# A delta rule loop by token halves: TensorE's order laid out by strands with dense products in their waits, norms by one-column products, a decay mask by a product

## Chip, cores and metric

The kernel runs on one core of one Trainium2 chip, in one launch. The metric is the device time of that core in microseconds (us), the median of several executions.

## What is computed

A trunk of two layers over 1024 tokens of width 1024, all in float32. Layer 0 mixes tokens with gated linear attention (GLA), layer 1 with a gated delta rule; behind each mixer stands a SwiGLU feed-forward part, and a root-mean-square norm stands ahead of each part and at the end. The change lies in the delta rule mixer:

```python
proj = h @ w_in
qkv, z, b, a = split(proj)
qkv = silu(causal_depthwise_conv(qkv, conv_w))
q, k, v = split(qkv)            # 8 heads of q and k, 16 of v, 128 wide
q, k = l2_norm(q), l2_norm(k)
...
# for each chunk of tokens, with S carried from chunk to chunk:
decay = exp(where(causal, G[:, None] - G[None, :], -inf))
A = where(strict, (kb @ k.T) * decay, 0)
T = triangular_solve(eye + A, eye)
v_new = T @ (v * beta) - (T @ (kb * exp(G))) @ S
o = (q * exp(G)) @ S + where(causal, (q @ k.T) * decay, 0) @ v_new
S = exp(G_last) * S + k_dec.T @ v_new
...
return (rms_norm(o, norm_w) * silu(z)) @ w_out
```

## The kernel before

**Precision.** A large product ("dense") takes each operand as a high and a low part in the fp32r type and makes three products of 512 columns, high by high, high by low and low by high (`mm3`, recorded at lines 153 to 155 whatever the stage). Weights come by DMA on SyncE's queue (SP) into a buffer `raw` (2), ScalarE casts the high part `whi` (line 122), GpSimd subtracts to get the low part `wlo` (line 123); there are 3 buffers for the split parts. Small products are plain fp32 and show as two records each.

**Units.** The delta rule stage, `gdn`, works in 16 units: two halves of 512 tokens by 8 head pairs, each with one q, one k and two v heads, and 4 chunks of 128 tokens. A half's normed input (`normx`) and its gates are made once. For each unit:

- *keys*, *values*, *late*: dense products of 24 each for q and k, v0 and v1, and the two halves of the gate z; q, k and v go through a convolution on VectorE (line 588) and a Silu on ScalarE.
- *prep*: products k by k (line 618), transposes of q (621), squares and norms from both (627, 628, `rsqrt`), the decay matrix dec (GpSimd makes rh at 654, TensorE multiplies it at 655, ScalarE takes Exp at 656, GpSimd multiplies by the triangular mask at 657), the score matrix nt (663, one buffer) and at (676, 678). Four diagonal blocks of nt go by DMA through DRAM into nbx (670, 672).
- *solve*: transposes of k and v (kt at 696, vt at 704), then 31 steps of two VectorE operations each (712, 714) that invert the diagonal blocks; the result goes by DMA through DRAM into xt (719, 722).
- *join*: four steps of products (737) with copies between them make the whole inverse tt (730 to 750, one buffer).
- *seq*: the recurrence over 4 chunks with the state gstate (766 to 813), where TensorE, VectorE and ScalarE alternate.
- *post*: a second `rsqrt`, transposes of o (825), the gate (`gateout`, lines 264 to 266); *out*: 48 dense products that are added to h (240).

**Order.** `pipeline` writes one iteration after another as a list of steps with offsets, here "solve+1 seq late+1 keys+2 out-1 prep+2 values+2 post join+1". The framework's scheduler then orders the instructions of every engine by its own estimate of when they are ready, in favour of those written first. On the chip each engine runs its instructions in that order, and waits where one isn't ready. At the end `ffnhead` begins the next feed-forward part ahead of the last unit's post.

PSUM is in three pools: `pd` (3 banks) for dense products, `pp` (2) for preparation, `pq` (3) for join, seq and post.

Of the kernel before, what the change touches and what calls it, by code (L numbers as in the profile page):

```python
# [32 lines left out]
HEAD = 3  # L33

# [17 lines left out]

class Trunk:
    def __init__(self, ctx, tc, a):
        self.ctx, self.tc, self.nc, self.a = ctx, tc, tc.nc, a
        nc = tc.nc
# [17 lines left out]
    def mixerpools(self, es):  # L74

        pool = lambda nm, n: es.enter_context(self.tc.tile_pool(name=nm, bufs=n))
        self.wr, self.ws, self.tp = pool("wraw", 2), pool("wsplit", 3), pool("units", 2)
        self.xs = self.tc.tile_pool(name="xhalf", bufs=1, side="right")
        self.xp = self.xs.__enter__()
# [17 lines left out]
    def loadrest(self):  # L97
# [13 lines left out]
        nc.vector.tensor_copy(self.gt, g)  # L111

# [37 lines left out]

    def mm3(self, ps, lhs, rhs, first, last, **kw):
        mm = self.nc.tensor.matmul
# [4 lines left out]
    def chan(self, ps, w, c0, x, ks=range(KT)):  # L157

        for k in ks:
            self.mm3(ps, [t[:, k, c0:c0 + P] for t in w], [t[:, k, :] for t in x], k == 0, k == ks[-1],  # L160
                     skip_group_check=ks[0] > 0)

# [6 lines left out]
    def rsqrt(self, s, n):  # L169
# [27 lines left out]
    def normx(self, half, w, pool, scratch, tag="jk"):  # L197

        nc = self.nc
        hi = pool.tile([P, KT, HT], F32R, name="xhi", tag="xhi")  # L200
        lo = pool.tile([P, KT, HT], F32R, name="xlo", tag="xlo")
        r = self.normr(half, lambda i: scratch.tile([P, HT], F32, name="jk", tag=tag, bufs=2))
        for k in range(KT):
# [3 lines left out]
            eng.tensor_tensor(out=xn, in0=src, in1=r.unsqueeze(2).to_broadcast([P, C, P]), op=ALU.mult)  # L207
            ps = self.prepps()
            for t in range(C):
                nc.tensor.transpose(ps[:, t * P:(t + 1) * P], xn[:, t, :], self.ident)  # L210
            self.split(hi[:, k, :], lo[:, k, :], ps, w[:, k:k + 1])
        return hi, lo
# [18 lines left out]
    def addout(self, half, w, lhs, cc):  # L231

        if True:
            for t in range(C):
                ps = self.dps()
                for k in range(2):
                    self.mm3(ps, [v[:, t * P:(t + 1) * P] for v in lhs[k]],
                             [v[:, k, :] for v in w], k == 0, k == 1)
                o = self.h[:, half * C + t, cc * 512:(cc + 1) * 512]
                self.nc.vector.tensor_tensor(out=o, in0=o, in1=ps, op=ALU.add)  # L240
# [13 lines left out]
    def outproj(self, half, w, r0, oT):  # L254
        for cc in range(2):
            self.addout(half, self.loadrows(w, r0, cc), oT, cc)
# [242 lines left out]
    def gdn(self, tail):  # L499
# [3 lines left out]
        NQ, B = 8, 32  # L503
        with ExitStack() as es:
            self.mixerpools(es)
# [22 lines left out]
            def gates(x):  # L528

                low = mx.tile([2 * B, HT], F32, name="low", tag="raw", bufs=2)  # L530
                S.copy(low, self.lowproj(w_in, 6 * D, B, x)[0:2 * B, :])
                ps = self.prepps()
                for t in range(C):
                    TE.matmul(ps[:, t * B:(t + 1) * B], low[:, t * P:(t + 1) * P], two, start=True, stop=True)
# [3 lines left out]
                tmp6 = mx.tile([P, 6, C, 16], F32, name="tmp6", tag="raw", bufs=2)  # L538
# [24 lines left out]
                flat = lambda t: t.rearrange("p c h -> p (c h)")  # L563
                ps = self.prepps()
                TE.matmul(ps[:, 0:64], self.upper, flat(g), start=True, stop=True)
# [603 lines left out]
```

## Time and profile before

| | |
|---|---|
| median of 3 runs | 3312.93 us (3312.15 to 3317.28) |
| profiled execution, its own time | 3317.64 us |
| profiled execution, span from first to last instruction | 3315.9 us |
| TensorE products busy / weight loads busy | 2979.9 us (90%) / 2422.4 us (73%) |
| VectorE / ScalarE / GpSimd busy | 2174.2 us (66%) / 1386.2 us (42%) / 1564.2 us (47%) |
| mean granted TensorE clock | 0.958 |

Times inside a profile are counted from the span's start. PE is TensorE's products, PEld its weight loads, DVE VectorE, ACT ScalarE, POOL GpSimd, SP the queue of SyncE that issues the DMAs. The granted clock is the mean of TensorE's two levels as a share of the full one: 1 is 2.4 GHz throughout, 0.5 would be 1.2 GHz throughout. The delta rule stage lies between about 1251 and 2690 us.

### The profile page before, as it was taken

The page shows a single profiled execution, that of the slowest core. Times are in us where ns is not written, and L with a number is a line of the kernel's source. Part 1 is how long each engine was busy: PE and PEld are TensorE (multiplying, and loading weights), DVE is VectorE, ACT ScalarE, POOL GpSimd, SP SyncE. Part 2 cuts the span into 40 slices and gives each one's busy share as a digit, 9 for nine tenths or more (in the row PEclk, how much of TensorE's full clock was granted, in tenths as well). Part 3 has the DMA queues.
Part 4 walks back from the last instruction along what each step waited for, and adds up shares of the span by engine and source line. Part 5 has one row for each costly group of instructions (what it writes and reads, how often), then busy time and mean ns, then how long its engine had stood idle before and what let it go on. Part 6 is the DMA issues. An engine that isn't in the chain of part 4 may idle for free. (4 is left out here: it accounts for less than half of the span.)

```text
span 3315.9 us, 40871 instructions
## 1 busy us (share of the span) xinstructions
PE 2979.9 (90%) x14323; PEld 2422.4 (73%) x14323; DVE 2174.2 (66%) x4493; ACT 1386.2 (42%) x2605; POOL 1564.2 (47%) x1069
## 2 busy tenths in 40 slices
PE   6988989799998999788898988899988889999898
PEld 5877877578886777677676766777776678887676
DVE  6465665633225996768888888888878542232998
ACT  5345444334343334444444544444444433333333
POOL 4344443455556874433333333333432355554885
PEclk9999999899999999899999999999999999999999
DMA  4222212322223312222222222222222232222331
GB/s 127 73 59 58 70 58 78 107 83 83 83 77 121 111 67 53 69 61 59 62 69 63 53 74 63 65 76 68 63 68 60 70 111 81 85 83 82 138 104 58
DMA packets 364924, 256.40 MB, mean 77 GB/s; under 512 B 67847, under 2 KB 309966, under 8 KB 364718
## 3 DMA queue, kind: packets, MB, share of 16 engines
q1 hardware_dynamic: 364654, 253.77, 25.8%
q8 instruction: 113, 1.85, 0.2%
q14 instruction: 93, 0.76, 0.1%
q0 software_dynamic: 64, 0.02, 0.0%
HBM read 219.12 MB, written 34.60 MB: 77 GB/s over the span
## 5 line engine op out<-in xcount | busy, mean ns | idle before, releaser
L123 POOL TENSOR_TENSOR wlo<-raw,whi 128x1024 fp32r<-128x1024 f32 x204 | 490.2, 2405 | 842.7 <-ACT whi L122 716.9
L153 PE MATMUL pd<-xhi,whi 128*128 128x512 f32 x1072 | 442.8, 414 | 0.9 <-ACT xhi L193 0.9
L154 PE MATMUL pd<-xlo,whi 128*128 128x512 f32 x1072 | 437.1, 408 | 0.0
L155 PE MATMUL pd<-xhi,wlo 128*128 128x512 f32 x1072 | 434.0, 405 | 0.0
L122 ACT CAST whi<-raw 128x1024 fp32r<-128x1024 f32 x204 | 214.0, 1049 | 295.0 <-issue 119.2
L895 POOL TENSOR_TENSOR olo<-s,ohi 128x512 fp32r<-128x512 f32 x152 | 195.9, 1290 | 206.1 <-ACT ohi L894 206.1
L895 POOL TENSOR_TENSOR olo<-raw,ohi 128x512 fp32r<-128x512 f32 x138 | 190.3, 1382 | 209.3 <-ACT ohi L894 181.7
L155 PEld LDWEIGHTS pd<-xhi,wlo 128*128 128x128 f32 x1072 | 205.6, 192 | 39.6 <-issue 0.3
L153 PEld LDWEIGHTS pd<-xhi,whi 128*128 128x128 f32 x1072 | 206.2, 193 | 38.7 <-ACT xhi L193 1.4
L154 PEld LDWEIGHTS pd<-xlo,whi 128*128 128x128 f32 x1072 | 206.6, 193 | 37.1
L153 PE MATMUL pd<-whi,ohi 128*128 128x512 f32 x384 | 164.5, 429 | 35.5 <-ACT k L586 22.5
L712 DVE TENSOR_TENSOR tmpx<-nbx,xix 128x60 f32<-128x60 f32 (+24 forms) x496 | 187.1, 377 | 9.9
L894 ACT CAST ohi<-s 128x512 fp32r<-128x512 f32 x152 | 94.3, 622 | 230.9 <-PE pd L154 172.9
L894 ACT CAST ohi<-raw 128x512 fp32r<-128x512 f32 x138 | 85.1, 621 | 197.9 <-POOL olo L895 176.0
L714 DVE TENSOR_TENSOR xix<-xix,tmpx 128x60 f32<-128x60 f32 (+24 forms) x496 | 160.9, 324 | 10.2
L154 PE MATMUL pd<-wlo,ohi 128*128 128x512 f32 x384 | 161.0, 419 | 0.0
L1051 POOL TENSOR_TENSOR blo<-t,bhi 128x1536 fp32r<-128x1536 f32 (+1 forms) x32 | 126.8, 3963 | 69.1 <-ACT bhi L1050 64.2
L155 PE MATMUL pd<-whi,olo 128*128 128x512 f32 x384 | 158.3, 413 | 0.9 <-DVE olo L266 0.9
L240 DVE TENSOR_TENSOR h<-h,pd 128x512 f32<-128x512 f32 x192 | 130.2, 682 | 44.0 <-PE pd L155 42.9
L1003 DVE TENSOR_TENSOR p<-p,pp 128x512 f32<-128x512 f32 x38 | 26.1, 688 | 197.5 <-DMA raw<-in_ffn_w_gate_up_dram 148.3
L153 PE MATMUL pd<-bhi,ahi 128*128 128x512 f32 x264 | 110.6, 419 | 36.7 <-DVE h L1061 21.3
L153 PEld LDWEIGHTS pd<-whi,ohi 128*128 128x128 f32 x384 | 76.0, 198 | 63.6 <-ACT k L586 27.2
(387 smaller groups left out, 8320.2 us busy)
## 6 DMA issues: line engine op xcount, KB each, us to landing
raw<-in_gdn_w_in_dram SPq DMA_DIRECT2D x96, 512.0 KB, 4.0
raw<-in_ffn_w_gate_up_dram SPq DMA_DIRECT2D x176, 256.0 KB, 3.3
raw<-in_gla_w_in_dram SPq DMA_DIRECT2D x48, 512.0 KB, 3.9
ra<-act SPq DMA_DIRECT2D x88, 256.0 KB, 5.1
rb<-in_ffn_w_down_dram SPq DMA_DIRECT2D x24, 768.0 KB, 6.5
raw<-in_gdn_w_out_dram SPq DMA_DIRECT2D x32, 512.0 KB, 4.2
act<-p SPq DMA_DIRECT2D x44, 256.0 KB, 2.0
act<-u SPq DMA_DIRECT2D x38, 256.0 KB, 2.0
```

What stands on the lines that cost most here:

```text
L122: nc.scalar.copy(hi, raw)
L123: nc.gpsimd.tensor_tensor(out=lo, in0=raw, in1=hi.bitcast(F32), op=ALU.subtract)
L153: mm(ps, lhs[0], rhs[0], start=first, stop=False, **kw)
L154: mm(ps, lhs[0], rhs[1], start=False, stop=False, **kw)
L155: mm(ps, lhs[1], rhs[0], start=False, stop=last, **kw)
L240: self.nc.vector.tensor_tensor(out=o, in0=o, in1=ps, op=ALU.add)
L712: V.tensor_tensor(out=tv, in0=nbx[:, s, s + 1:].unsqueeze(2).to_broadcast([P, n, w]), in1=xv[:, s:s + 1, 0:w].to_broadcast([P, n, w]), op= ...
L714: V.tensor_tensor(out=xv[:, s + 1:, 0:w], in0=xv[:, s + 1:, 0:w], in1=tv, op=ALU.add)
L894: self.nc.scalar.copy(hi, src)
L895: eng.tensor_tensor(out=lo, in0=src, in1=hi.bitcast(F32), op=ALU.subtract)
L1003: V.tensor_tensor(out=p1, in0=p1, in1=pb, op=ALU.add)
L1051: eng.tensor_tensor(out=lo, in0=src, in1=hi.bitcast(F32), op=ALU.subtract)
```

## The change

- `pipeline` is no longer used by the delta rule stage. Each kind of step becomes a generator (a strand) that runs over all 16 units and yields either a time to wait or an `Event` that another strand sets. `Order.run` plans: it keeps a clock which each product advances by its assumed length, takes the strands in the order seq, post, join, prep, inputs (gates and norms), solve whenever one is due, and otherwise three dense products. Within `manual_schedule` TensorE issues its instructions in just the order in which they are written; the order on the other engines stays with the scheduler.
- The transposes of k and v move from solve to the first chunk of seq; products k by k move behind the decay; xt's way and the start of a unit's scores wait, in the plan, for the join of the unit before.
- tt gets two buffers; split weights of this stage go from 3 buffers to 2.
- The norms of q and k: a square of the whole tile on ScalarE and 8 fp32 products with one column of ones, in place of 4 transposes of q and 8 accumulating operations on ScalarE and VectorE.
- The decay: the mask is added ahead of Exp by a product of -65536 times the identity with a strictly triangular matrix, in place of GpSimd's multiplication behind it.
- `rsqrt`, in the whole kernel: one step of higher order and one of the old kind, 9 operations in place of 11.
- `ffnhead` for the second layer becomes dense work (`headparts`) at the end of the same plan.

```diff
+class Order:
+    def set(self, e, after=0.0):
+        e.at = self.clock + after
+    def run(self, strands, dense):
+        live = [[g, 0.0] for g in strands]
+        fill = [dense, 0.0]
+        def go(x):
+            r = x[1].at if isinstance(x[1], Event) else x[1]
+            if r is None or r > self.clock:
+                return False
+            v = next(x[0], "end")
+            if v == "end":
+                x[0] = None
+            else:
+                x[1] = v if isinstance(v, Event) else self.clock + (v or 0.0)
+            return True
+        while live or fill[0]:
+            if any(go(x) for x in live):
+                live = [x for x in live if x[0]]
+            elif not (fill[0] and go(fill)):
+                ...
+                self.clock = max(self.clock, min(at)) + 0.01
...
+        nc.vector.tensor_scalar(out=self.cut, in0=self.ident, scalar1=MASKED, scalar2=None, op0=ALU.mult)
...
+    def mm(self, out, lhsT, rhs, start=True, stop=True, **kw):
+        n = int(np.prod(out.shape[1:]))
+        self.order.clock += n * 0.00044 + 0.003 if lhsT.dtype == F32R else max(n * 0.00169, 0.05) + 0.008
+        self.nc.tensor.matmul(out, lhsT, rhs, start=start, stop=stop, **kw)
...
-        for _ in range(3):
-            nc.vector.tensor_tensor(out=t, in0=y, in1=y, op=ALU.mult)
-            nc.vector.scalar_tensor_tensor(out=t, in0=t, scalar=-0.5, in1=s, op0=ALU.mult, op1=ALU.mult)
-            nc.vector.scalar_tensor_tensor(out=y, in0=t, scalar=1.5, in1=y, op0=ALU.add, op1=ALU.mult)
+        r = 0.375 ** 0.5
+        V.tensor_tensor(out=t, in0=y, in1=y, op=ALU.mult)
+        V.scalar_tensor_tensor(out=t, in0=t, scalar=r, in1=s, op0=ALU.mult, op1=ALU.mult)
+        V.scalar_tensor_tensor(out=t, in0=t, scalar=-1.25 / r, in1=t, op0=ALU.add, op1=ALU.mult)
+        V.scalar_tensor_tensor(out=y, in0=t, scalar=1.875, in1=y, op0=ALU.add, op1=ALU.mult)
+        V.tensor_tensor(out=t, in0=y, in1=y, op=ALU.mult)
+        V.scalar_tensor_tensor(out=t, in0=t, scalar=-0.5, in1=s, op0=ALU.mult, op1=ALU.mult)
+        V.scalar_tensor_tensor(out=y, in0=t, scalar=1.5, in1=y, op0=ALU.add, op1=ALU.mult)
...
-            self.mixerpools(es)
+            self.mixerpools(es, 2)
...
+            def dense():
+                yield from keys(0)
+                yield from values(0)
+                yield from late(0)
+                yield from keys(1)
+                yield from late(1)
+                yield from keys(2)
+                yield from values(1)
+                for m in range(1, UN):
+                    yield from values(m + 1)
+                    if m + 2 in (NQ, UN):
...
+                    else:
+                        yield from keys(m + 2)
+                        yield from out(m - 1)
+                        yield from late(m + 1)
+                yield ready[2]
+                yield from self.headparts(1, mx, ("v", "v", "raw"))
+                yield from out(UN - 1)
...
-                for c in range(C):
-                    sl = slice(c * P, (c + 1) * P)
-                    TE.transpose(pq[:, sl], q[:, sl], self.ident)
...
-                    S.activation(j0, pq[:, sl], AF.Square, accum_out=s8[:, 0, c:c + 1])
-                    V.scalar_tensor_tensor(out=j1, in0=pk[:, sl], scalar=1.0, in1=self.ident, op0=ALU.mult,
-                                           op1=ALU.mult, accum_out=s8[:, 1, c:c + 1])
+                for i, nm in enumerate("qk"):
+                    sq = mx.tile([P, C, P], F32, name="sq", tag="t2", bufs=2)
+                    S.activation(sq.rearrange("p c i -> p (c i)"), u[nm], AF.Square)
+                    yield 1.5
+                    for c in range(C):
+                        self.mm(ps[:, i * C + c:i * C + c + 1], sq[:, c, :], self.ones[:, 0:1])
...
+                    self.mm(psv, self.cut, self.gt.unsqueeze(1).to_broadcast([P, C, P]), True, False)
+                    self.mm(psv, self.gt, rhs[0], False, False)
+                    self.mm(psv, self.gt, rhs[1], False, True)
                     S.activation(dec[:, h2].rearrange("p c i -> p (c i)"), ps, AF.Exp)
-                    G.tensor_tensor(out=dec[:, h2], in0=dec[:, h2], in1=up, op=ALU.mult)
+                yield 1.5
+                if n:
+                    yield joined[n - 1]
...
+                O.set(scored[n], 4.0)
...
+            def solve(n):
+                half = n % 2
+                yield scored[n]
...
+                yield 6.0
+                start = O.clock + 0.75
...
+                    yield O.until(start + 0.75 * s)
+                if n:
+                    yield joined[n - 1]
...
+                O.set(solved[n], 8.0)
+            def join(n):
+                yield solved[n]
+                if n >= 2:
+                    yield passed[n - 2]
...
+                tt = mx.tile([P, 8, P], F32, name="tt", tag="tt", bufs=2)
...
-            self.pipeline(
-                [(half, hq) for half in range(2) for hq in range(NQ)],
-                "solve+1 seq late+1 keys+2 out-1 prep+2 values+2 post join+1",
...
+            with self.tc.manual_schedule(engines={mybir.EngineType.PE}):
+                O.run([each(seq), each(post), each(join), each(prep), inputs(), each(solve)], dense())
```

## Rows read from the trace of the kernel before

**Rows 1.** The page, part 1: busy us (share of the span) x instructions.

```profile
PE 2979.9 (90%) x14323; PEld 2422.4 (73%) x14323; DVE 2174.2 (66%) x4493; ACT 1386.2 (42%) x2605; POOL 1564.2 (47%) x1069
```

**Rows 2.** Busy time by stretch: length, PE, PEld, DVE, ACT, POOL, clock, DMA share, GB/s.

```profile
690.00:1251.00 561.00, 539.05 (x2323) 440.99 (x2322) 296.00 (x284) 205.91 (x285) 354.18 (x184) 0.98 0.27 89
1251.00:1410.00 159.00, 131.12 (x606) 105.78 (x604) 111.29 (x247) 67.98 (x109) 72.08 (x75) 0.90 0.25 64
...
1862.00:1958.00 96.00, 82.60 (x419) 63.53 (x417) 84.64 (x223) 45.14 (x99) 38.07 (x35) 0.95 0.23 59
...
2038.00:2504.00 466.00, 417.59 (x2125) 333.72 (x2125) 378.71 (x1002) 213.06 (x498) 166.49 (x154) 0.96 0.25 67
...
2630.00:2690.00 60.00, 44.36 (x178) 33.20 (x178) 44.69 (x73) 26.00 (x45) 16.25 (x10) 0.87 0.37 105
```

**Rows 3.** Instructions of line 730: count, shortest/median/longest ns, first and last start.

```profile
L730 ACT COPY tt<-xt x16: 1037/1046/1052, 1398.8 to 2565.0; 128x1024 f32<-128x1024 f32 x16
```

**Rows 4.** Time line of TensorE: start us, length us, operation, count.

```profile
1688.72 0.39 PE L154 MATMUL pd<-xlo,whi 128*128 128x512 f32 x1
...
1690.99 0.39 PE L155 MATMUL pd<-xhi,wlo 128*128 128x512 f32 x1
...
1692.90 1.06 PE L737 MATMUL pq<-xd,nt 128*128 128x128 f32 x8
...
1699.75 1.57 PE L737 MATMUL pq<-xt,rr 128*96 128x96 f32 x16
...
1294.98 1.08 PE L534 MATMUL pp<-two,low 64*128 64x32 f32 x8
```

**Rows 5.** Waits of TensorE from 2038 to 2504 us: total us, times, longest.

```profile
PE pq L737 <- DVE sz L264: 15.1, 6, 2.7
PE pd L153 <- ACT k L586: 11.9, 6, 2.2
PE pq L782 <- DVE rt L771: 6.8, 6, 1.9
PE pq L766 <- DVE gstate L796: 4.6, 3, 1.5
```

**Rows 6.** Time lines of VectorE, SP, ScalarE and TensorE through one unit's chain.

```profile
2028.85 2.15 DVE L663 SCALAR_TENSOR_TENSOR nt<-pp,nb,dec 128x128 f32<-128x128 f32 x8
...
2034.10 1.71 SPq L672 DMA_DIRECT2D nbx<-d  x4
...
2043.36 0.29 DVE L712 TENSOR_TENSOR tmpx<-nbx,xix 128x31 f32<-128x31 f32 x1
...
2071.03 0.17 DVE L714 TENSOR_TENSOR xix<-xix,tmpx 128x8 f32<-128x8 f32 x1
...
2079.45 1.05 ACT L730 COPY tt<-xt 128x1024 f32<-128x1024 f32 x1 [2.16 <-DMA xt<-d]
...
2096.59 1.06 PE L737 MATMUL pq<-xd,nt 128*128 128x128 f32 x8
...
2112.39 0.41 DVE L750 TENSOR_TENSOR tt<-tt,pq 64x256 f32<-64x256 f32 x1 [0.63 <-PE pq L737]
```

**Rows 7.** Groups of instructions from 2038 to 2504 us, on VectorE and GpSimd: busy us, mean ns.

```profile
L180 DVE TENSOR_TENSOR rs_t<-rs_y 128x8 f32<-128x8 f32 x36 | 21.8, 638 | 0.0
L182 DVE SCALAR_TENSOR_TENSOR rs_y<-rs_t,rs_y 128x8 f32<-128x8 f32 x36 | 18.9, 559 | 0.0
...
L628 DVE SCALAR_TENSOR_TENSOR jk<-pp,cst 128x128 f32<-128x128 f32 x24 | 6.8, 284 | 0.6
...
L123 POOL TENSOR_TENSOR wlo<-raw,whi 128x1024 fp32r<-128x1024 f32 x48 | 114.7, 2390 | 221.3 <-ACT whi L122 161.3 <-PE pq L802 57.3 <-issue 1.9
L657 POOL TENSOR_TENSOR dec<-dec,cst 128x512 f32<-128x512 f32 x12 | 15.6, 1299 | 0.3 <-ACT dec L656 0.3
```

**Rows 8.** Waits of GpSimd from 2038 to 2504 us.

```profile
POOL wlo L123 <- PE pq L802: 57.3, 9, 8.0
```

**Rows 9.** Time line of VectorE: first and last operation of an early unit's solve.

```profile
1420.41 0.18 DVE L712 TENSOR_TENSOR tmpx<-nbx,xix 128x31 f32<-128x31 f32 x1
...
1460.79 0.16 DVE L714 TENSOR_TENSOR xix<-xix,tmpx 128x8 f32<-128x8 f32 x1
```

More of the change, by code (lines that the diff above doesn't have):

```diff
@@ L33 @@
 HEAD = 3
+MASKED = -65536.0
 def shape_constants():
@@ L50, with __init__, until @@
 NCONST = (3 + NMASK) * P + HT
+class Event:
+    at = None
+class Order:
+    def __init__(self):
+        self.clock = 0.0
+    def set(self, e, after=0.0):
+        e.at = self.clock + after
+    def until(self, t):
+        return max(t - self.clock, 0.0)
+    def run(self, strands, dense):
[15 more added lines that the diff above has]
+            elif not (fill[0] and go(fill)):
+                at = [x[1].at if isinstance(x[1], Event) else x[1] for x in live + [fill] if x[0]]
+                at = [t for t in at if t is not None]
+                assert at, "strands wait for one another"
+                self.clock = max(self.clock, min(at)) + 0.01
 class Trunk:
@@ new lines, in out, with norm, inputs @@
+            def out(n):
+                if 0 <= n < UN:
+                    yield posted[n]
+                    half, hq = divmod(n, NQ)
+                    yield from self.outparts(half, w_out, hq * 256, U[n]["oT"])
+            def norm(half):
+                x.clear()
+                yield from self.normparts(x, half, self.mixw[1], self.xp, mx, "raw")
+            free, ready = [Event() for _ in range(3)], [Event() for _ in range(3)]
+            def inputs():
+                yield from gates(x, 0)
+                yield free[1]
+                yield from norm(1)
+                O.set(ready[1], 1.0)
+                yield from gates(x, 1)
+                yield free[2]
+                yield from self.normparts(self.head, 0, self.ffnw[1], self.xp, mx, "raw")
+                O.set(ready[2], 1.0)
@@ L829, in gdn @@
-            self.pipeline(
-                [(half, hq) for half in range(2) for hq in range(NQ)],
-                "solve+1 seq late+1 keys+2 out-1 prep+2 values+2 post join+1",
-                norm=lambda half: self.normx(half, self.mixw[1], self.xp, *((mx, "raw") if half else (self.tp, "vch"))),
-                gates=gates, proj=proj, late=late, prep=prep, solve=solve, join=join, seq=seq,
-                post=lambda o, u: post(o, u["z"]),
-                wout=lambda half, hq, oT: self.outproj(half, w_out, hq * 256, oT), tail=tail)
+                    self.turn(ps, lambda c: o[:, c, h2, :])
@@ L845, in ffnhead, with each @@
+                    u["oT"].append(self.gateout(mx, h2, ps, self.gdnw, u["z"][:, h2, :]))
+                O.set(posted[n], 4.0)
+            def each(f):
+                for n in range(UN):
+                    yield from f(n)
+            for _ in norm(0):
+                pass
+            with self.tc.manual_schedule(engines={mybir.EngineType.PE}):
+                O.run([each(seq), each(post), each(join), each(prep), inputs(), each(solve)], dense())
     def ffnhead(self, l):
+        self.head = self.normx(0, self.ffnw[l], self.xp, self.tp, "vch")
```

360 lines of the change are left out of this document (226 added, 134 removed).

## The prediction, as it was made before the result

> **What bounds the kernel now.** I read the page's engine totals first, then the busy time of each engine by stretch, then the waits of TensorE and the time lines of the stretch that the change rewrites. The page alone misleads: TensorE is busy 90% of the span [rows 1], so it looks as if nothing were left. The table by stretch says more. In the SwiGLU stretch from 690 to 1251 us TensorE is busy 539 of 561 us at a granted clock of 0.98; in the delta rule stretch, from 1251 to about 2690 us, it is at 0.90 at the start, 0.95 at the change of token half, 0.96 in the steady part and 0.87 at the end [rows 2]. And "busy" counts the overlapping tails of pipelined products, so the delta rule stretch has to be counted by start-to-start times.
>
> The 16 units (8 head pairs, two halves) follow each other every (2565.0 - 1398.8) / 15 = 77.7 us, by the first and last copy of xt [rows 3]. What one unit asks of TensorE I count from the code and price by pitches [rows 4]:
> - 192 dense products of 512 columns (48 each for keys, values, gate and output): ten steps from 1688.72 to 1690.99 make 0.227 us each, so 43.6 us.
> - A 128-column fp32 product is two records; eight records take 1.06 us, and without the length of the last (0.275) that is 0.112 each. 64 records (k by k, k by q, first join step, tt and at of the recurrence): 7.2 us. 24 records of 256 columns at twice that: 5.4. 32 of 96 columns, from sixteen in 1.57 us, 0.088 each: 2.8. 16 of 64 columns at 0.06: 1.0. 24 transposes at 0.11: 2.6. Four 512-column products for the decay: 0.9.
>
> Sum 63.5 us. So 14.2 us of each unit are not products. Six units fit into 2038 to 2504 us. There TensorE's listed waits add up to 47.8 us in ten rows, 8.0 a unit; the four largest are shown [rows 5]. The granted clock of 0.96 [rows 2], a mean of 1.2 and 2.4 GHz, loses 4%, 3.1 us. The last 3.1 us are short gaps where TensorE goes from one kind of product to another. VectorE is the second engine to watch: 378.7 us in those 466, 63.1 us a unit [rows 2].
>
> Why do the waits arise? Follow one unit [rows 6]: nt is written from 2028.9 to 2031.0; the loads of nbx are issued until 2035.8; the 31-step solve starts at 2043.4 and ends at 2071.2 on VectorE; xt has landed by 2079.45, when ScalarE copies it; but TensorE takes up the join only at 2096.6, 17 us later, since it stands behind the transposes of post in TensorE's order, and join ends at 2112.8. The unit's chain waits for TensorE's order, and the order for the chain.
>
> **The change, part by part.** Sums are against the profiled execution, 3317.6 us with a span of 3315.9; the runs' median is 3312.9, 4.7 less, and I take the difference of the sum off the median.
>
> *TensorE's work.* Gone are 4 transposes of q a unit (0.44 us). Added are two 512-column products with cut (0.46) and 8 one-column products. No such product is in the trace. Bounds: below nothing; above, the 32-column fp32 product, whose eight records take 1.08 us, 0.115 each [rows 4]. It is the nearest row, so 16 records make 1.8 us. I take that. Products: 63.5 + 1.8 = 65.3 us.
>
> *TensorE's order.* It is now written by a planner with a clock: strands (seq, post, join, prep, inputs, solve) go first, dense products three at a time when no strand is due. Its latencies are near what I read: 4.0 after the k products and 6.0 more until the solve, against 2.15 + 4.8 + a landing of about 2.5 (the xt copy starts 2.5 us after its last issue); 0.75 a solve step against 27.8 / 31 = 0.90 with other work between; 8.0 against 8.3 for the way to xt [rows 6]. So join stands where xt lands, and dense products fill. What goes: the waits for sz (15.1 us in six units) and for the bank that ACT k frees (11.9), as join no longer follows post. What stays: waits inside the recurrence and the join, for rt and gstate (6.8 and 4.6) and in two rows not shown 5.3, together 16.7, 2.8 us a unit. I leave them in full: strands make them shorter, but VectorE's queue is fuller (below), and a planned due time that comes early holds all of TensorE. The short gaps stay (3.1). The clock falls after waits; with 2.8 of 8.0 us left I leave 1.0 of its 3.1. Unit: 65.3 + 3.1 + 2.8 + 1.0 = 72.2 us, 5.5 less, over 15 intervals 83 us. Bounds: no waits, no clock loss, one-column products for nothing: 66.6; nothing gained: 77.7 plus the 1.8.
>
> *VectorE.* The four accumulating products with the identity are removed (6.8 us in six units, 1.1 a unit [rows 7]); each rsqrt has 9 small operations where it had 11, and the two that go are one of the kind that takes 638 ns on the mean here and one of the kind that takes 559 [rows 7]: 1.2 us a call, 2.4 a unit. 63.1 becomes 59.6, which fits under 72.2 (83%). This work lay beside TensorE's dense products; I price it at nothing, and at its 3.5 us if VectorE were the bound. Outside the stretch rsqrt lies on the path at some ten places (norms at stage edges, five at the end): two operations each, 3 us if they take 0.16 us as the shortest here do, and up to 6 at the means above; I take 3.
>
> *GpSimd's mask.* Two multiplications of 1.30 us a unit go [rows 7]; one of them lay between Exp and nt. Hidden behind the dense products, taken as nothing. The small VectorE operations that last 638 ns here stand beside GpSimd's work. The Trainium skill, "SBUF — State Buffer", Who interferes with whom, says that a VectorE instruction with two SBUF inputs and a GpSimd one that reads SBUF block each other for the whole instruction; by that rule up to 2.6 us more a unit would come back to VectorE, and the chain of the first rival would be that much shorter. The sum above goes without it.
>
> *Start, half and end.* From 1251 to 1410 us, 159 us, the clock of 0.90 costs 16 us, and gates now run as a strand beside the first keys instead of ahead: I take 12 (0 to 28). The interval with the second half's norm is 96 us [rows 2], 18 over the mean, of which some 8 are products of its own; half of the other 10 goes: 5. The end, with the head of the next SwiGLU as dense work for the last unit, was filled that way before: 5 (0 to 10).
>
> *Buffers and queues.* tt gets a second buffer, split weights two instead of three. SP's queue keeps the same transfers; the eight of a solve still share it with weight loads, whose wait for a raw buffer stands ahead of them as before.
>
> Sum: 83 + 3 + 12 + 5 + 5 = 108 us. 3312.9 - 108 = 3205 us.
>
> **The rivals.**
> - *The unit's chain stays the bound.* nt has one buffer, so each unit's chain follows the last one's. With the steps of [rows 6]: nt 2.1, way to the solve 12.4, solve 27.8, way to xt 8.3, join about 11 and the k products with their wait 2.4, 64 us: under 72. But in the early units, where join was prompt, the solve took from 1420.4 to 1461.0, 40 us [rows 9], since other VectorE work stood between its steps; then it is 76.6 us, 1.1 a unit less than now, 16 in all, and with the 25 us of the other terms 3272 us. For it: VectorE must do 59.6 us of work in a shorter unit. Against: the steps are given out one by one at the planner's pace, so later work stands behind them.
> - *Two split buffers hold TensorE* (slower). A tile's split may start only when the tile two before it is used up, and must end within one tile's 24 products, 5.5 us when dense. GpSimd's part alone is 2.39 us [rows 7], and it waited up to 8.0 us in nine cases for TensorE to pass products of the recurrence [rows 8]; with three buffers that never reached TensorE, whose ten rows of waits hold none for wlo. From 0.9 us a tile on (8 tiles a unit, against the 7.2 us a unit that all terms give) the kernel is slower; at 2.0 us it is 8 x 2.0 - 7.2 = 8.8 a unit, 3312.9 + 132 = 3445; at 1.5, 3385. Against: a tile takes 72 / 8 = 9 us on the mean, not 5.5.
> - *All waits and clock losses go*: 66.6 a unit, 11.1 less, 167 us, with 28 at the start and the rest 13: 3105 us.
> - *The order changes nothing*, since VectorE, whose order is not fixed by hand, sets it anyway: 3313 + 1.8 x 15 - 20, about 3320.
>
> **How the numbers follow.** Forecast 0.58, at 3205, from 3140 to 3260 alone. Chain bound 0.16. Split buffers, or hand-set waits like them, 0.12. All gone 0.11. No change 0.03. Of the chain case a sixth I count as no measurable change. A measurement here tells 0.2%, 6.6 us. Faster: 0.58 + 0.11 + 0.13 = 0.82; same 0.06; slower 0.12. The range is 3115 to 3305: it leaves out the slower cases and half of the fastest one.
>
> **What would show it.** Right: copies of xt every 72 us; the join's first product within 2 us of that copy; TensorE's waits for sz and the bank gone; clock 0.98 or more in the steady part; VectorE near 60 us a unit. Wrong: dense products that wait for wlo (split buffers); a solve of 40 us with join waiting for xt (the chain); the eight one-column products taking much more or less than 1.8 us; new waits of TensorE for rt or vt larger than the ones gone.

## The result, and the profile after

The changed kernel is slower: 3477.96 us (median of four runs, 3477.36 to 3483.76) against 3315.11 us for the kernel before on the same chip, a ratio of 1.0494 (95% interval 1.0476 to 1.0512). Forecast were 3205 us, range 3115 to 3305. The profiled execution has a span of 3476.3 us, 160.4 more than before.

The page's engine totals, which answer to [rows 1]:

```profile
PE 3016.6 (87%) x14547; PEld 2482.9 (71%) x14547; DVE 2065.9 (59%) x4212; ACT 1390.3 (40%) x2513; POOL 1522.6 (44%) x1037
```

VectorE and GpSimd do less than before (108 and 42 us) and TensorE only 37 us more, while the span is 160 us longer: most of the time went into waiting. Where, the copies of xt say, one a unit (count, shortest, median and longest ns, first and last start), beside [rows 3]:

```profile
L907 ACT COPY tt<-xt x16: 1044/1046/1053, 1398.7 to 2706.6; 128x1024 f32<-128x1024 f32 x16
```

The first copy comes as early as before. From first to last it takes 1307.9 us instead of 1166.2, 87.2 a unit instead of 77.7: 141.7 of the 160.4 us. After the last copy 769.7 us remain instead of 750.9, 18.8 more. Busy time by stretch (as in [rows 2]): the start of the stage, an early unit, a steady unit, the unit with the change of half, five units of the second half, the stage after.

```profile
1251.00:1410.00 159.00, 128.61 (x608) 104.46 (x607) 93.38 (x215) 67.47 (x97) 62.25 (x68) 0.89 0.23 60
...
1411.00:1474.00 63.00, 39.99 (x226) 33.84 (x225) 43.71 (x139) 24.69 (x60) 11.15 (x19) 0.78 0.14 32
1651.00:1740.00 89.00, 73.38 (x370) 60.47 (x369) 58.22 (x155) 34.56 (x74) 26.38 (x29) 0.90 0.21 58
1917.00:2057.00 140.00, 116.12 (x581) 94.07 (x580) 96.91 (x260) 65.91 (x153) 40.19 (x39) 0.91 0.20 53
2123.00:2556.00 433.00, 360.10 (x1843) 298.21 (x1842) 288.43 (x771) 176.90 (x383) 131.75 (x125) 0.92 0.22 59
...
2850.00:3476.00 626.00, 584.90 (x2520) 478.07 (x2520) 325.83 (x376) 231.16 (x338) 379.63 (x202) 0.97 0.27 90
```

Five regular units take 433 us, 86.6 each. VectorE is busy 57.7 of them, so neither it nor TensorE is full. By the starts of nt, the score matrix of a unit, the fifteen intervals are of three kinds: three of 63 to 66 us (the first two units and the first of the second half), eleven of 85.5 to 88.7, and one of 139.5 with the change of half. Who waits in the five regular units? TensorE's waits (us in total, times, longest; to set beside [rows 5]), then VectorE's:

```profile
PE pq L207 <- DVE o L1035: 21.5, 5, 4.3
PE pq L201 <- DVE xd L906: 20.9, 5, 4.2
PE pd L201 <- DVE tmpx L883: 14.9, 5, 3.2
PE pq L201 <- DVE rt L976: 8.5, 5, 1.8
```

```profile
DVE tt L925 <- PE pq L201: 44.8, 10, 8.7
DVE tt L934 <- PE pq L201: 31.6, 5, 6.3
```

Each waits for the other. TensorE's six listed rows add up to 73.0 us (two of 3.7 and 3.5 are not shown), 14.6 a unit; VectorE stands 76.4 us, 15.3 a unit, at the two adds of the join. No row says that TensorE waits for wlo. One regular unit shows how it goes (VectorE with one row of SP's queue, then TensorE and ScalarE; start, length, the idle time ahead in brackets):

```profile
1650.91 2.16 DVE L841 SCALAR_TENSOR_TENSOR nt<-pp,nb,dec 128x128 f32<-128x128 f32 x8 [0.73 <-PE pp L201]
...
1656.22 1.71 SPq L868 DMA_DIRECT2D nbx<-d  x4
...
1661.52 3.42 DVE L692 SCALAR_TENSOR_TENSOR v<-raw,col_conv,v 128x512 f32<-128x512 f32 x3 [2.86 <-ACT v L690]
...
1667.01 0.18 DVE L883 TENSOR_TENSOR tmpx<-nbx,xix 128x31 f32<-128x31 f32 x1
...
1697.62 3.45 DVE L1035 TENSOR_TENSOR o<-o,rs_y 128x512 f32<-128x512 f32 x2
...
1705.75 0.17 DVE L885 TENSOR_TENSOR xix<-xix,tmpx 128x8 f32<-128x8 f32 x1
...
1718.12 1.25 DVE L906 STREAM_TRANSPOSE xd<-xt 128x1024 f32<-128x1024 f32 x1
1727.62 0.55 DVE L925 TENSOR_TENSOR tt<-tt,pq 96x384 f32<-96x384 f32 x1 [8.25 <-ACT sz L720]
...
1736.49 0.88 DVE L934 TENSOR_TENSOR tt<-tt,pq 64x256 f32<-64x256 f32 x2 [6.99 <-PE pq L201]
...
1739.57 2.16 DVE L841 SCALAR_TENSOR_TENSOR nt<-pp,nb,dec 128x128 f32<-128x128 f32 x8 [0.73 <-PE pp L201]
...
1700.61 1.94 PE L207 MATMUL pq<-cst,o 128*128 128x128 f32 x8 [4.24 <-DVE o L1035]
...
1709.09 0.95 PE L201 MATMUL pp<-ones,sq 128*128 128x1 f32 x8
...
1719.42 2.08 PE L201 MATMUL pq<-xd,nt 128*128 128x128 f32 x8 [4.90 <-DVE xd L906]
...
1726.67 0.84 PE L201 MATMUL pq<-xt,rr 128*96 128x96 f32 x8
...
1735.78 1.15 PE L201 MATMUL pq<-ya,rr 96*64 96x64 f32 x16
...
1713.29 1.05 ACT L907 COPY tt<-xt 128x1024 f32<-128x1024 f32 x1 [1.07 <-DMA xt<-d]
```

Read it against [rows 6]. The last load of nbx is issued by 1657.9 and these loads land 2.7 us after their issue, yet VectorE begins the solve only at 1667.01, behind operations of the recurrence and the taps of v (the multiply-adds of the convolution), for which it has to wait. During the solve VectorE has work almost without a break, the solve itself and between its steps the taps of v, k and q, the adds to h, the scaling of o: the solve takes 38.9 us (27.8 before). In the same time TensorE has used up what stands ahead of the join in its fixed order and waits at o and xd. xt is copied at 1713.29, yet VectorE reaches xd only at 1718.12, behind the small operations of the norms. Then it turns round: from 1719.42 on TensorE has work, the dense products laid between the steps of the join, and VectorE stands 8.25 and 6.99 us at the adds of the join (the first row names ScalarE's sz, but the product that the add reads ends at 1726.67 + 0.84 = 1727.51, just ahead of it). The join takes 18.0 us from its first product, where an early unit takes 9. nt then follows 2.2 us after its end.

The change of half (from the first 512 tokens to the second), on VectorE: nt of the last unit, the second half's norm (its first sum of squares), nt of the first unit after; first the kernel before, then the changed one.

```profile
1853.35 2.15 DVE L663 SCALAR_TENSOR_TENSOR nt<-pp,nb,dec 128x128 f32<-128x128 f32 x8
1858.43 0.68 DVE L225 SCALAR_TENSOR_TENSOR jk<-h 128x512 f32<-128x512 f32 x1
...
1948.15 2.16 DVE L663 SCALAR_TENSOR_TENSOR nt<-pp,nb,dec 128x128 f32<-128x128 f32 x8
```

```profile
1917.03 2.30 DVE L841 SCALAR_TENSOR_TENSOR nt<-pp,nb,dec 128x128 f32<-128x128 f32 x8 [0.73 <-PE pp L201]
1942.37 0.68 DVE L301 SCALAR_TENSOR_TENSOR jk<-h 128x512 f32<-128x512 f32 x1
...
2056.50 2.16 DVE L841 SCALAR_TENSOR_TENSOR nt<-pp,nb,dec 128x128 f32<-128x128 f32 x8 [0.94 <-PE pp L201]
```

The interval is 139.5 us instead of 94.8, 44.7 more: the norm starts 25.3 us after nt instead of 5.1, and from the norm to the next nt it takes 114.1 us instead of 89.7.

### The profile page after: what moved, and what is told of

Its sections match the earlier page's. It is cut to its first block, busy times and chain, and to the rows that moved or that the text cites. A ratio compares the mean times of both kernels' runs of the same rounds, so it can differ in the third digit from the quotient of the medians.

```text
span 3476.3 us, 40951 instructions
## 1 busy us (share of the span) xinstructions
PE 3016.6 (87%) x14547; PEld 2482.9 (71%) x14547; DVE 2065.9 (59%) x4212; ACT 1390.3 (40%) x2513; POOL 1522.6 (44%) x1037
## 4 chain that ended last, share of the span: by engine, by line
PE 63%; DVE 26%; issue 4%; DMA 3%; ACT 2%; POOL 1%; SPq 1%; DVEq 0%; POOLq 0%; ACTq 0%
PE pd L201 36%; PE pq L201 14%; PE pp L201 8%; DVE tmpx L883 4%; DVE xix L885 3%; DVE alo L1274 2%; DVE h L1284 1%; DVE s L1268 1%; PE pp L207 1%; DVE v L692 1%; PE pp L484 1%; PE pq L207 1%; DVE k L692 1%; DMA ra<-act 1%; DVE q L692 1%
## 5 line engine op out<-in xcount | busy, mean ns | idle before, releaser
L201 PE MATMUL pd<-xhi,whi 128*128 128x512 f32 x1072 | 458.6, 428 | 1.2 <-ACT part L1082 0.9
L201 PE MATMUL pd<-xlo,whi 128*128 128x512 f32 x1072 | 428.2, 399 | 0.0
L883 DVE TENSOR_TENSOR tmpx<-nbx,xix 128x60 f32<-128x60 f32 (+24 forms) x496 | 177.7, 358 | 8.5
L885 DVE TENSOR_TENSOR xix<-xix,tmpx 128x60 f32<-128x60 f32 (+24 forms) x496 | 153.2, 309 | 8.7
L201 PE MATMUL pq<-xd,nt 128*128 128x128 f32 x256 | 57.3, 400 | 114.0 <-DVE xd L906 114.0
```

The costliest lines, as they stand in the source:

```text
L201: self.nc.tensor.matmul(out, lhsT, rhs, start=start, stop=stop, **kw)
L883: V.tensor_tensor(out=tv, in0=nbx[:, s, s + 1:].unsqueeze(2).to_broadcast([P, m, w]), in1=xv[:, s:s + 1, 0:w].to_broadcast([P, m, w]), op= ...
L885: V.tensor_tensor(out=xv[:, s + 1:, 0:w], in0=xv[:, s + 1:, 0:w], in1=tv, op=ALU.add)
```

## The experiments

The theories are named anew in each set. All kernels compute the whole of the reference. Times are medians beside runs of the kernel before on the same chip (3313.8 to 3316.1 us).

**First set: parts alone, order alone, two links of the chain alone.**

The small parts (norms by one-column products, mask by a product, nine operations for rsqrt) put into the kernel before, with its pipeline kept (inside prep the k by k products move behind the decay, as in the changed kernel):

```
-  TE.transpose(pq[:, sl], q[:, sl], self.ident)
...
+  TE.matmul(pn[:, i * C + c:i * C + c + 1], sq[:, c, :], self.ones[:, 0:1], start=True, stop=True)
...
-  G.tensor_tensor(out=dec[:, h2], in0=dec[:, h2], in1=up, op=ALU.mult)
+  TE.matmul(cview(ps), self.cut, self.gt.unsqueeze(1).to_broadcast([P, C, P]), start=True, stop=False)
```

> The kernel before with the arithmetic parts of the change alone: rsqrt in 9 operations, norms by one-column products, the decay's mask by a product; the old pipeline order, three split buffers and one tt buffer. If these parts are no cause of the loss (both theories): 3313 less 0 to 30 us, since VectorE gives up some 3.5 us a unit and GpSimd 2.6. If the one-column products cost much more than their 1.8 us a unit: above 3330 us.

3306.29 us, ratio 0.9978 (0.9968 to 0.9987). The parts gain 7 us and cost nothing in the old order. So the loss lies in what is left, the new order of work with its buffers.

The changed kernel with the one line taken out that fixes TensorE's order; strands, planner and the order of emission stay:

```
-  with self.tc.manual_schedule(engines={mybir.EngineType.PE}):
-      O.run([each(seq), ...
+  O.run([each(seq), ...
```

> The changed kernel without the fixed order of TensorE: the same instructions are written in the same order, but the scheduler may order TensorE's as before. Theory 1 (the wait for the whole join, which holds only while TensorE's order is fixed): the k products go ahead of the join again, and the time comes back to 3300 to 3360 us. Theory 2 (the plan's order is good, and VectorE's order, which the scheduler sets in either case, makes the loss): 3440 us or more.

3293.51 us, ratio 0.9936 (0.9918 to 0.9954): 0.6% below the kernel before, and 184 us faster than with the fixed order. Theory 1 had 3300 to 3360 here, theory 2 3440 or more; the time lies 6.5 us below theory 1's range. Its copies of xt, TensorE's wait for xd over the loop (114.0 us, 16 times, in the changed kernel), VectorE's waits at the join in six units from 2018 to 2467 us, and one unit (nt, the end of its solve, the join's first product, the next nt, the join's last adds):

```profile
L907 ACT COPY tt<-xt x16: 1027/1041/1053, 1396.6 to 2532.3; 128x1024 f32<-128x1024 f32 x16
```

```profile
PE pq L201 <- DVE xd L906: 9.9, 5, 4.3
```

```profile
DVE tt L934 <- PE pq L201: 10.8, 8, 3.6
...
DVE tt L925 <- PE pq L201: 8.3, 8, 3.4
```

```profile
2017.93 0.87 DVE L841 SCALAR_TENSOR_TENSOR nt<-pp,nb,dec 128x128 f32<-128x128 f32 x3 [0.33 <-PE pq L201]
...
2074.61 2.33 DVE L885 TENSOR_TENSOR xix<-xix,tmpx 128x8 f32<-128x8 f32 x1
...
2086.30 2.05 PE L201 MATMUL pq<-xd,nt 128*128 128x128 f32 x16 [0.24 <-DVE xd L906]
...
2088.40 0.87 DVE L841 SCALAR_TENSOR_TENSOR nt<-pp,nb,dec 128x128 f32<-128x128 f32 x3 [2.15 <-PE pq L201]
...
2093.28 0.73 DVE L934 TENSOR_TENSOR tt<-tt,pq 64x256 f32<-64x256 f32 x2
```

First to last copy 1135.7 us, 172.2 less than in the changed kernel. The change of half is still long, 131.9 us by the starts of nt; the other fourteen are 60 to 82 us, 70.8 on the mean, next to the 72.2 forecast. VectorE's waits at the join fall from 15.3 to 3.2 us a unit, though its solve still takes 33 to 43 us in all but the first unit of each half.

The two units shown tell where the loss lies. In the changed kernel the interval of 88.7 us is made of 55.0 from nt to the end of the solve, 13.5 from there to the join's first product, 18.0 for the join and 2.2 from its end to the next nt. Under the scheduler's order the 70.5 us are 59.0, 9.4, 7.7 and -5.6: the next nt stands ahead of the join's end again, as in the kernel before. So it is not the long solve that makes the loss; in this pair of units all of it lies behind the solve. One caution: with the line VectorE's order changes too (nt is now written as three operations and five, with adds of the join between them). The experiment shows what the fixed order costs, not what TensorE's part of it costs by itself.

The k products of the next unit after the first step of the join, not after its end; and the 62 operations of the solve with a higher priority for VectorE's scheduler; both with the fixed order:

```
-  yield joined[n - 1]
+  yield freed[n - 1]           # set after quad(nt, xd, 1)
```

```
+  with self.tc.high_priority():
       V.tensor_tensor(out=tv, ...); V.tensor_tensor(out=xv[:, s + 1:, 0:w], ...)
```

> The changed kernel, but the k by k products of a unit wait in the plan only for the first step of the join before (the last reader of nt), not for the whole join. Theory 1: the chain of a unit (scores, solve, join) sets the 88 us a unit, and the wait for the whole join put 12 us into it, since nt is now written 2 to 3 us after the join's end and was written 8 to 10 us ahead of it before. Then nt starts some 8 us before the join's end, a unit takes about 77 us and the kernel about 3478 - 14 x 10 = 3340 us (3310 to 3370). Theory 2: TensorE's own waits for xd and its half clock set the time and the chain has slack. Then less than 15 us changes.

> The changed kernel, but the 62 operations of each solve have the scheduler's highest priority, so that VectorE runs them whenever they are ready. Theory 1 with the solve's stretch from 27.8 to 38.9 us as its second cause: the solve takes 22 to 27 us, a unit about 77 us, the kernel about 3340 us (3310 to 3380), even though the other VectorE work comes later. Theory 2 (TensorE's waits set the time): the solve gets shorter, but rt, gstate and the bank releases come later and the time stays within 20 us of 3478 or rises.

3447.56 us (1.0404, 1.0388 to 1.042) and 3481.5 us (1.0505, 1.0489 to 1.0521). The first gains 30 us: theory 1 had 3310 to 3370 and theory 2 less than 15 us of change, so neither number came, and theory 1 falls for the most part. The second gains nothing, but its solve stays at 37 to 38 us in the regular units, so it does not tell what a short solve would do.

**Second set: is the chain stretched by the join and by the clock of the order?** The pauses in the join were set to zero (`yield 0.5`, `1.5` and `1.2` to `yield 0.0`), so that no dense products lie in it; to that were added the early k products; or a clock that gives the solve 1.0 us a step and xt 10 us; or both.

```
-  yield O.until(start + 0.75 * s)      +  yield O.until(start + 1.0 * s)
-  O.set(solved[n], 8.0)                +  O.set(solved[n], 10.0)
```

> The changed kernel with the planned pauses inside join set to zero, so that the join's products follow each other in TensorE's fixed order with no dense products laid between them. Theory A (the unit's chain is the bound, and the fixed order has stretched the join from 9 to 18 us, since 18.7 us of other products were planned into it): the join falls to about 9 us and the unit from 88 to about 79, some 9 us in each of 13 units, about 3360 us. Theory B (TensorE stands still because its fixed order runs ahead of VectorE's queue; a stretch cut in one place comes back as a wait in another): join falls, the wait for xd or a wait inside the join grows by as much, 3440 us or more.

> As the run before, and the k products of the next unit wait only for the first step of the join and not for its end (that alone gave 30 us). Theory A: the two cuts add, about 3330 us, the unit near 77 us. Theory B: no further gain, 3410 us or more.

> Zero pauses in the join as above, and the order's clock takes 1.0 us for a step of the solve instead of 0.75, and 10 us instead of 8 for the way from the solve to xt, nearer to the 38 us that 31 steps take, so that more dense products are laid ahead of the join's first product. Theory A: the same dense products lie where TensorE stood still; the wait for xd (114 us in the changed kernel) falls below 60 and the time to about 3330. Theory B: with the planned join behind the real one the wait for xd goes too, but the chain is longer by what the join is now late, so no better than the tight join alone.

> Tight join, k products after the join's first step, and the slower clock for the solve together. Theory A: about 3310 us, level with the kernel before, the unit near 75 us, half change still about 130 us. Theory B: 3400 us or more.

3497.8 (1.0553, 1.0537 to 1.0568), 3475.63 (1.0486, 1.047 to 1.0501), 3446.04 (1.0398, 1.0381 to 1.0416) and 3433.94 us (1.0359, 1.0343 to 1.0374). Theory A fell: with the tight join the join does take 8.4 to 9.5 us, but from its end to the next nt it now takes mostly 10 to 17 us instead of 2.2, TensorE's wait for xd grows, and the kernel is slower. TensorE's waits of that kernel from 1400 to 2760 us:

```profile
PE pq L201 <- DVE xd L906: 140.9, 15, 25.1
PE pq L207 <- DVE o L1035: 70.0, 15, 7.3
```

The dense products taken out of the join stand behind it, ahead of the k products, and ahead of xd there is nothing more to do. The early k products gain 22 us over the tight join alone. The slower clock, which moves dense products ahead of the join, gains 52, and the wait for xd falls to 58.3 us. Theory B had the times of the first, second and fourth kernel on its side, but it gave the third no gain at all over the first, so it is not right as it stood. The 52 us speak for an order that has TensorE at the join too early. Even so the regular units still take 82 to 86 us in that kernel, with solves of 43 to 47 us where the changed kernel's take 38 to 39.

**Third set: v turned early, and the solve's priority, under either order.** In the changed kernel v is turned inside the recurrence, after the join; here it gets a strand of its own, which waits for the values, the k products and the recurrence before.

```
+  def turnv(n):
+      yield valued[n]; yield scored[n]
+      if n: yield passed[n - 1]
+      u["vt"] = vt = ...            # the transposes and the two multiplications, moved here from seq
+      O.set(turned[n])
-  O.run([each(seq), ...             +  O.run([each(turnv), each(seq), ...
```

> The changed kernel, fixed order kept, with v turned in a strand of its own as early as above. Theory H: the change of half shortens by some 25 us and nothing else does, about 3450 us, which makes the change of half a second and separate loss beside the 13 long units. Rival: with the fixed order the gain is taken up by waits elsewhere, 3478.

> The changed kernel with TensorE's order left to the scheduler (3293.5 us) and v turned in a strand of its own, as soon as sk is there and the recurrence before has ended, instead of inside the recurrence after the join. Theory H (the change of half is long, 132 us against 95 before, because the last values of the half wait for v of the unit before to be turned, which now comes after its join, and the second half's norm and keys wait for those values): the interval with the change of half falls by some 25 to 30 us and the time to about 3265. Rival (the change of half is long since all of its products lie between the same two units): no change, 3293.

> TensorE's order left to the scheduler, with the 62 VectorE operations of the solve given a higher priority; v turned inside the recurrence as in the changed kernel. Theory C (in this version the unit's chain is the bound, and the solve of about 40 us is its longest part since other VectorE work stands between its steps): the solve falls to about 28 us, the unit from 71 to about 66 (TensorE's own products are then the bound), some 14 x 5 = 70 us, about 3225. Rival (with the fixed order the same priority did nothing): no change, 3293.

> Both of the above: scheduler's order, v turned early, solve with priority. If theories H and C both hold, about 3195 us; with H alone 3265; with neither 3293.

With the fixed order 3370.99 us (1.0171, 1.0154 to 1.0188), 107 us faster than the changed kernel, where theory H gave some 28 and a gain at the change of half alone. Under the scheduler's order 3307.9 (0.9982, 0.9972 to 0.9992), 3303.89 (0.9965, 0.9952 to 0.9978) and 3305.12 us (0.9965, 0.9952 to 0.9978): none better than the 3293.5 without them. The priority leaves the solve at 32 to 45 us in the regular units and gains nothing there either; theory C's gain did not come, but neither did its short solve. The kernel with early v and fixed order, at the change of half and in one solve:

```profile
1885.89 0.68 DVE L301 SCALAR_TENSOR_TENSOR jk<-h 128x512 f32<-128x512 f32 x1
...
1906.29 2.16 DVE L841 SCALAR_TENSOR_TENSOR nt<-pp,nb,dec 128x128 f32<-128x128 f32 x8 [0.65 <-PE pp L201]
...
1993.35 2.15 DVE L841 SCALAR_TENSOR_TENSOR nt<-pp,nb,dec 128x128 f32<-128x128 f32 x8
...
1677.56 0.18 DVE L883 TENSOR_TENSOR tmpx<-nbx,xix 128x31 f32<-128x31 f32 x1
...
1704.85 0.17 DVE L885 TENSOR_TENSOR xix<-xix,tmpx 128x8 f32<-128x8 f32 x1
```

The norm now starts 20.4 us ahead of nt, and the interval is 87.1 us, 52 less, twice the 25 of theory H. The solve takes 27.5 us, since the taps and the adds to h have left it; but the regular units go down only from 85.5-88.7 to 77-84 us. Under the scheduler's order early v shortens the change of half as well (132 to 89.5 us) and lengthens the other units from 70.8 to 76.3 us on the mean.

**Fourth set: the tight join again with early v, and the split buffers.** The last kernel is the one before with `pool("wsplit", 2)` in this stage instead of 3.

> Fixed order, v turned in its own strand (3371 us, unit 82, solve 27.5, first join product to join end 16 to 20) and the pauses inside the join at zero. Theory A2 (with v out of the way the chain of the unit bounds, so the join's stretch now counts, which it did not while VectorE's work stood in the solve): the join falls to 9 us, the unit to about 74, the time to about 3270. Rival B (a stretch taken out of one place comes back as a wait, as in the earlier run with zero pauses, which was 18 us slower): 3360 or more.

> As the first of these, and the k products of the next unit wait for the join's first step alone. Theory A2: a further 5 us a unit off the chain until TensorE's 65 us bound, about 3220. Rival B: no gain over the first.

> The same with TensorE's order left to the scheduler (with v in its own strand and the pauses kept: 3308 us, unit 78, join 16). Theory A2: join 8, unit about 71, 3308 - 14 x 7 = about 3210. Rival B: 3300.

> The kernel before with two buffers of split weights instead of three in the delta rule stage, nothing else. The rival that named these buffers as the loss expects 0.9 us or more for each of 128 tiles, 115 us slower, about 3430; the trace of the changed kernel, where TensorE waits 4.4 us in all for wlo, lets expect 3315 to 3330.

3457.11 (1.0419, 1.0403 to 1.0434), 3461.83 (1.0431, 1.0416 to 1.0447), 3318.22 (1.0007, 0.9998 to 1.0017) and 3314.74 us (0.9998, 0.9988 to 1.0009). The tight join costs 86 us with the fixed order: TensorE's wait for xd goes from 57.3 back to 112.0 us, the change of half to 143.8, and the solve, 27.5 us without it, is back at 34 to 46 in ten of the sixteen units. Under the scheduler's order it loses 10 us. Theory A2 fell like A. Two split buffers cost nothing in the kernel before.

**Fifth set: v early in one unit alone**, the one before the last of the first half, to tell the change of half from the rest.

```
+  EARLY = (NQ - 2,)                 # turnv(n) for these in a strand, for the others in seq
```

> TensorE's order left to the scheduler (3293.5 us, units of 71 us, change of half 132 us), and v turned early in one unit alone, the one before the last of the first half, on which the values that hold back the second half's norm depend. Theory H: the other units keep their 71 us, the change of half falls by some 40 us as it did with v early in all units (89 us), the time to about 3255, the fastest here. Rival: the gain at the change of half is taken up elsewhere (units longer), 3290 or more.

> The same one early turn in the changed kernel with its fixed order. Theory H: the change of half falls by some 50 us, the units of 88 us stay, about 3428 us; so of the 107 us that v early in all units gave, half is the change of half and half the solve that no longer has the v taps between its steps. Rival: as with v early in all units, 3371, since one early turn shifts the whole order; or no gain, 3478.

3290.51 us (0.9937, 0.9923 to 0.9951) and 3474.91 us (1.0486, 1.0472 to 1.0501). The first has the lowest time here, but only 3 us below the version without early v, which their intervals don't tell apart, and not the some 40 of theory H. The change of half stays at 130.9 and 137.7 us. With the fixed order its norm starts at 1936.10, 20.1 us after nt (1916.02), only 5 earlier. The first of the half's last two values on ScalarE, in the changed kernel, in this one with the fixed order, and in the one with the fixed order and v early in all units:

```profile
1931.12 0.63 ACT L694 ACTIVATE v<-v 128x512 f32<-128x512 f32 x1 [2.52 <-DVE v L692]
```

```profile
1929.41 0.63 ACT L694 ACTIVATE v<-v 128x512 f32<-128x512 f32 x1 [2.06 <-DVE v L692]
```

```profile
1878.01 0.63 ACT L694 ACTIVATE v<-v 128x512 f32<-128x512 f32 x1 [2.69 <-DVE v L692]
```

v of the unit before is turned 51 us earlier here than in the changed kernel (1864.1 instead of 1915.0), and the last values come 1.7 us earlier. So it is not that one wait which holds them. With v early in all units the dense products stand so far ahead that the last values come 28 us before nt (1906.29), and the norm comes with them; theory H holds in that wider form alone, and why all units are needed for it is not shown.

## Why the prediction was wrong, point by point

**The step that failed** is "TensorE's order": "So join stands where xt lands, and dense products fill", with waits of 2.8 us a unit. In the unit shown the join's first product comes 6.1 us after the copy of xt, and the waits are 14.6 us a unit. The clock, taken as 1.0 us of loss, is 0.92 granted, a mean of 1.2 and 2.4 GHz, 8% of 86.6, 6.9 us. With products at 65.1 these make the 86.6 measured, where the forecast was 72.2. The prediction's 3.1 us of short gaps would come on top, so part of the clock's loss must lie in the waits: the terms show the size, not a clean sum.

Behind it stands a comparison of latencies that were not near. The order allows 4.0 + 6.0 + 31 x 0.75 = 33.3 us from the k products to the end of the solve. I set its 4.0 + 6.0 beside 2.15 + 4.8 + 2.5, the way to the landing of nbx, and left out what VectorE does first: by [rows 6] it is 14.5 us from nt to the solve's first operation and 42.3 to its last, and the first rival was worked out with these very figures. In the changed kernel nt to solve's end takes 2.2 + 4.8 + 9.1 + 38.9 = 55.0 us. [rows 9] had shown the 40 us solve of units with a prompt join, and I used it for a rival only.

**What took its place**, shown by the one-line experiment: with the same emission and no fixed order the units take 70.8 us on the mean and the kernel 3293.5. The fixed order costs 184 us. It places TensorE's products by a clock that counts no VectorE queue, while VectorE's queue is in another order, that of the scheduler. Both take their instructions one after the other, so TensorE idles while VectorE ends its stretch, and VectorE idles while TensorE makes up the dense products in the join. The traces show both kinds of idle time; that a cut in one place comes back in another, four kernels with a tight join show. That the missing VectorE queue in the clock is the reason rests on the 52 us from a slower clock, and is beyond that argued. The Trainium skill, "PSUM — Partial Sum Buffer", Engine vs sequencer instructions, says that VectorE's and ScalarE's queues are strictly first in, first out, and that products start and complete in program order; the trace agrees: xt had landed by 1713.29, and xd stood behind the norms until 1718.12.

**The change of half** was to gain 5 us and lost 44.7. I priced it as an interval with some more products, not as a chain that starts with the norm. In the plan the norm waits for the half's last values and gate products, the values for v of the unit before, and v is now turned behind that unit's join; I had not followed that.

**VectorE**: 59.6 us a unit forecast, 57.7 measured. The size was right. What the account left out is the place: much of this work now lies between the steps of the solve.

**The small terms.** One-column products: eight records take 0.95 us, without the last length (0.25) 0.100 each, 1.6 us a unit against the 1.8 taken, which makes the products 65.1. The parts together gain 7 us where they stand alone. The waits of [rows 5] that the sum kept or dropped are 43.7 of the 47.8 us; 4.1, 0.7 a unit, fell out without a word. At the start 12 us were forecast: the first copy comes at 1398.7, as before, so none. At the end 5: the stretch after the last copy is 18.8 us longer, and 12 of it is the last unit's join (19.5 us instead of 7.3).

**The rivals.** The chain as the bound (3272 us): its solve of 40 us came, but a tighter join did not shorten the unit, so it isn't the bound by its sum. Two split buffers (slower): the sign came, the mechanism did not; no row of five regular units has TensorE wait for wlo, and in the kernel before two buffers cost nothing. No waits at all and no change both fell with the time. Of the signs, no row of these units has the waits for sz and for the bank that k frees, and VectorE is near 60 us a unit, while the copies come every 87 us and the clock is 0.92. The sentence that named the danger, "a planned due time that comes early holds all of TensorE", stood beside 16.7 us of waits that I left as they were; it should have been a rival of its own with [rows 9] as its price.

**Still open**: why early v and the scheduler's order don't add (the units go from 70.8 to 76.3 us on the mean), and what holds the unit at 77 to 84 with early v and the fixed order. In the changed kernel the three intervals of 63 to 66 us are the ones with both a solve of 23 to 28 us and a join under 10; no kernel here has both throughout, so what the two together would give is not shown. Fixing VectorE's order together with TensorE's was not tried.

## What to carry to other kernels

An order written out for one engine alone is only as good as its clock's picture of the other engines' queues: compare its latencies with the time from the trace at which the other engine really takes up the work, not with the landing of its input, and with a unit in which the consumer is already prompt. Before judging such a change, take out the one line that fixes the order; here it separated 184 us of order from the rest. And where two in-order engines idle in turn, shortening one link moves the wait; look for whether both have idle time in the same unit.

## What the runs showed of the hardware

A VectorE operation of 0.2 us can take as long as the GpSimd split beside it. In the changed kernel, VectorE and GpSimd in the same solve:

```profile
1668.26 0.19 DVE L885 TENSOR_TENSOR xix<-xix,tmpx 128x29 f32<-128x29 f32 x1
1668.48 2.32 DVE L883 TENSOR_TENSOR tmpx<-nbx,xix 128x28 f32<-128x28 f32 x1
...
1668.37 2.39 POOL L169 TENSOR_TENSOR wlo<-raw,whi 128x1024 fp32r<-128x1024 f32 x1 [4.96 <-ACT whi L168]
```

The product tmpx started 0.11 us after the split and ended at 1670.80, 0.04 after it. The Trainium skill, "SBUF — State Buffer", Who interferes with whom, says that a VectorE instruction with two inputs in SBUF and a GpSimd instruction that reads SBUF exclude each other for the whole instruction; this pair agrees. Four of the splits fall into this solve; three of them hold a solve operation of 0.2 to 0.3 us, for 2.32, 2.20 and 2.38 us, and the fourth the scaling of o.
